# Forgetting attention in a two-layer decoder step: scores of two more heads ahead of a head's transposes, and the samples' bias in steps

## The chip, the cores and the metric

The kernel runs on one core of one Trainium2 chip. The time is device microseconds of one execution. TensorE (PE) multiplies matrices into PSUM, VectorE (DVE) and ScalarE (ACT) read PSUM and work element by element, GpSimd (POOL) works in SBUF, and SyncE (SP) holds most of the DMA queue.

## The reference

One inference step of a two-layer trunk for a prompt of 512 tokens and a group of 8 samples with 4 tokens each (544 columns in all), width 1024, float32. Layer 0 is Mamba-2 heads beside sliding-window attention; layer 1, which the change touches, is forgetting attention. Each layer ends with cross-attention into 256 memory tokens and a SwiGLU FFN. Cut to what matters here:

```python
q, k, v, logf = odd_split(hp @ w_in_odd[li], fox_fb[li])      # 16 query heads, 4 key/value heads, width 64
cum = jnp.cumsum(logf, axis=1)
bias = cq[..., :, None] - c[..., None, :]                     # logit[t,s] += cum[t] - cum[s], causal mask
p = jax.nn.softmax(s * d ** -0.5 + bias, axis=-1)             # per block of 128 queries
o = jnp.einsum('...kgqs,...skd->...qkgd', p, v)
...
kp = cache_fox_k[li, page_table]                              # samples: 8 pages of 128 keys each, gathered
lp = cache_fox_logf[li, page_table]
cum = jnp.cumsum(jnp.concatenate([lp, logf], axis=1), axis=1)
```

## The kernel before, in words

Activations lie transposed, 128 rows of the width on the partitions. A product in float32 is made of three fp32r matmuls: weights and activations are split into a high and a low part (`acc3`), and a weight piece that a DMA has put into `room` is split by ScalarE (L161, high part) and VectorE (L162, low part) into `split_t`. `linear_steps` is a generator: one step is one output piece of 128 rows for one half of the columns (256 or 288), 24 matmuls.

In `odd` the keys, values and gates are projected, then `fox_keys` stacks high and low parts of the keys with the cumulated gates (kh, kl). `fox_bias` makes the samples' bias from the cache: it gathers the log gates of 64 pages by an indirect DMA (lg), transposes them on TensorE (16 transposes) to LTS by ScalarE copies (L1169), sums them by matmuls against ones and against a strict triangle (L), adds the later pages' totals (`late`, seven small VectorE additions), and splits the result into S. Before, all of that is written ahead of the query projection of heads 0 to 7 (`linear(wq, range(4), ...)`).

`fox_prompt(q, K2, V, m, c)` then handles one block of 128 queries (c) for 8 heads (m): a head's scores are two matmuls into a PSUM bank ("sc", two banks; from the 33rd head on also one of the three "tr" banks), VectorE adds the mask, writes the result to one of four buffers in `prt` and takes the minimum (L1135), ScalarE takes the exponential and the sum (L1136), VectorE the reciprocal (L1137), GpSimd the scaling (L1138). TensorE transposes the probabilities (tag "tp", two banks), VectorE or ScalarE copy them to PT (L1144), and after eight heads TensorE multiplies them with V. There are 64 such heads, with 128 to 512 keys.

Between the heads stand steps of three other generators, by the table `FOX_PLAN`: "q" the other half of the query projection, "s" the samples' attention in four groups of two samples (`fox_sample`, whose pages of keys and values SP loads by an address from the page table, 16 DMAs of 128 KB each), and "m" the memory's keys and values for cross-attention. After them comes the output projection (wd_o).

The order that is written is a priority. A scheduler that plays the program through puts every engine's instructions in the order that stands in the program, so an engine's order differs from the written one.

Of the kernel before, what the change touches and what calls it, by code (L numbers as in the profile page):

```python
# [9 lines left out]
F32 = mybir.dt.float32  # L10
F32R = mybir.dt.float32r
# [8 lines left out]
P = 128  # L20
D = 1024
KD = 8
# [13 lines left out]
FGROUPS = ((0, 4), (4, 4), (8, 4), (12, 4), (16, 6))  # L36
NEG = -1e30

FOX_PLAN = {}
for _a, _heads in (("q", range(4, 33, 4)), ("s", [33,34,36,38,40,41,43,45,47,49,51,53,55,57,59,61]), ("m", range(34, 64, 4))):  # L40
    for _h in _heads:
# [64 lines left out]
class Net:  # L106
# [880 lines left out]
    def odd(self, st, nxt, fill):  # L987
        nc, tc, I, O = self.nc, self.tc, self.I, self.O
        with ExitStack() as es:
# [23 lines left out]
            klast = self.last  # L1013
# [28 lines left out]
            wq = self.pieces(I["wd_q"], KD)  # L1042
            with tc.tile_pool(name="fox", bufs=1) as fx:
                self.pvs = []
                self.qst, self.prt = fx.tile([P, 4352], F32R, name="qst"), fx.tile([P, 4736], F32, name="prt")
                self.fsel = self.qst[:, 4096:4352]
                self.qs_at = self.pr_at = 0
                K2 = self.fox_keys(kT, ncum)
                S, sel = self.fox_bias(fx, klast)
                self.linear(wq, range(4), KD, xh, xl, qe)  # L1050
                self.take(q)
                self.banks = ['sc']
                gens = {"q": self.linear_steps(wq, range(4, 8), KD, xh, xl, qe),
                        "s": self.fox_sample(q, kTs, Qb, ncs, V, lf, fx, S, sel), "m": fill()}
                next(gens["s"])
                heads = 0
                for m in range(2):
                    for c in range(4):
                        for _ in self.fox_prompt(q, K2, V, m, c):
                            heads += 1  # L1060
                            self.banks = ['sc'] if heads < 33 else ['sc', 'sc', 'tr']
                            for a in FOX_PLAN.get(heads, ""):
                                next(gens[a], None)
                for a in "qsm":
                    for _ in gens[a]:
                        pass
                self.hold = self.whold = self.pvs[5]
                oh, ol = Big(self, "oh1", F32R), Big(self, "ol1", F32R)
                for c in range(2):
                    o, N = CH[c]  # L1070
                    for j in range(8):
                        last = self.split(oh, ol, q[j][:, o:o + N], j, o, N)
                self.x_load(self.xd, last)
                self.cross_keys(1, last)
                st2 = nxt()
                self.linear(self.pieces(I["wo_d"], KD), range(8), KD, oh, ol, self.x_evac(st2), tail=2, lead=3)
                self.hold = self.whold = None
        return st2

    def fox_keys(self, kT, ncum):  # L1080
# [14 lines left out]
        for j in range(2):  # L1095
            Q = self.qst[:, 2048 + 1024 * j:3072 + 1024 * j].rearrange("p (r i t) -> p r i t", r=2, i=4)
            for r in range(2):
                b = 64 - 64 * r
                d = nc.vector.tensor_copy(Q[b:b + 64, r], self.cst[0:64, C_OH:C_OH + 4].unsqueeze(2).to_broadcast([64, 4, 128]))
                self.after(d, self.last)  # L1100
        mask = self.prt[:, 4224:4736]
        self.zero(mask[:, 0:384])
        self.after(nc.gpsimd.tensor_copy(mask[:, 384:512], self.cst[:, C_SWA + 128:C_SWA + 256]), self.last)
        return kh, kl
# [11 lines left out]
            nc.vector.tensor_tensor(Q[0][b, r], src, Q[0][a, r].bitcast(F32), ALU.subtract)  # L1116
        return Q

    def fox_prompt(self, q, K2, V, m, c):
        nc = self.nc  # L1120
        W = 128 * (c + 1)
        tok = slice(128 * c, 128 * c + 128)
        Q = self.fox_queries(q, m, tok)
        PT = [self.H("PT")[:, 0:2048].rearrange("p (k r i t) -> p k r i t", k=2, r=2, i=4) for _ in range(c // 2 + 1)]
        mask = self.prt[:, 4736 - W:4736]
        for r in range(2):
            for i in range(4):
                sc = self.bank([P, 512])
                for z in range(2):
                    self.mm(sc[:, 0:W], Q[z][:, r, i], K2[z][:, m, r, 0:W], z == 0, z == 1)  # L1130
                nm, den, rec = self.ty(1), self.ty(1), self.ty(1)
                self.pr_at = (self.pr_at + 512) % 2048
                pr = self.prt[:, self.pr_at:self.pr_at + 512]

                nc.vector.tensor_tensor_reduce(pr[:, 0:W], sc[:, 0:W], mask, -1.0, 1e30, ALU.add, ALU.min, nm)  # L1135
                nc.scalar.activation(pr[:, 0:W], pr[:, 0:W], AF.Exp, bias=nm, scale=-1.0, accum_out=den)  # L1136
                nc.vector.reciprocal(rec, den)  # L1137
                nc.gpsimd.tensor_scalar(pr[:, 0:W], pr[:, 0:W], rec, 1.0, ALU.mult, ALU.mult)  # L1138
                tp = self.psum("tp", [P, 4, 128])
                for kb in range(c + 1):  # L1140
                    self.tr(tp[:, kb], pr[:, 128 * kb:128 * kb + 128])
                for u in range(c // 2 + 1):
                    e = min(2, c + 1 - 2 * u)
                    (nc.scalar.copy if i % 2 else nc.vector.tensor_copy)(PT[u][:, 0:e, r, i], tp[:, 2 * u:2 * u + e])  # L1144
                yield
        pv = self.psum("pv", [P, 4, 128])
        for kb in range(c + 1):
            for r in range(2):
                g = 2 * m + r
                self.mm(pv[64 * r:64 * r + 64], V[:, kb, 64 * g:64 * g + 64], PT[kb // 2][:, kb % 2, r], kb == 0, kb == c)  # L1150
        self.pvs.append(nc.vector.tensor_copy(q.half(m)[:, :, tok], pv))  # L1151

    def fox_bias(self, fx, last):

# [3 lines left out]
        lg = self.H("lg")[0:64, 0:2048]  # L1158
        nc.gpsimd.indirect_dma_start(out=lg, out_offset=None, in_=I["fox_logf"],
                                     in_offset=bass.IndirectOffsetOnAxis(ap=pg.bitcast(U32), axis=0))  # L1160
        ll = self.H("LTS")
        LT, suf = ll[:, 0:1024], ll[:, 1024:2048]
        L4 = LT.rearrange("p (g b h) -> p h b g", g=8, b=8)
        for u in range(2):
            tp = self.psum("tp", [P, 8, 64])
            for h in range(8):
                hh = 8 * u + h
                self.tr(tp[:, h], lg[:, 128 * hh:128 * hh + 128], 64)
            nc.scalar.copy(L4[:, 8 * u:8 * u + 8], tp.rearrange("p h (b g) -> p h b g", g=8))  # L1169

        pt = self.psum("tp", [P, 8])
        for g in range(8):
            self.mm(pt[:, g:g + 1], LT[:, 128 * g:128 * g + 128], self.ones[:, 0:1], True, True)
        tot, late = (fx.tile([P, 8], F32, name=n) for n in ("tot", "late"))
        nc.vector.tensor_copy(tot, pt)
        self.after(nc.vector.memset(late, 0.0), last)
# [2 lines left out]
        for u in range(2):  # L1179
# [3 lines left out]
                self.mm(tp[:, g], LT[:, 128 * x:128 * x + 128], self.L, True, True)  # L1183
            sv = suf[:, 512 * u:512 * u + 512].rearrange("p (g k) -> p g k", g=4)
            nc.vector.tensor_tensor(sv, tp, late[:, 4 * u:4 * u + 4].unsqueeze(2).to_broadcast([P, 4, 128]), ALU.add)
        S = self.H("S", F32R)[:, 0:2048].rearrange("p (s k) -> p s k", s=2)
        for r in range(2):
            a, b = slice(64 * r, 64 * r + 64), slice(64 - 64 * r, 128 - 64 * r)
# [2 lines left out]
        sel = self.fsel.rearrange("p (a t) -> p a t", t=4)  # L1191
        i2 = self.ident[:, 0:64].unsqueeze(2).to_broadcast([P, 64, 4]), self.ident[:, 64:128].unsqueeze(2).to_broadcast([P, 64, 4])
        self.after(nc.vector.tensor_tensor(sel, i2[0], i2[1], ALU.add), last)
        return S, sel.rearrange("p a t -> p (a t)")

    def fox_sample(self, q, kTs, Qb, ncs, V, lf, fx, S, sel):

# [25 lines left out]
        for G in range(4):  # L1223
# [9 lines left out]
            for b2 in range(2):  # L1233
# [3 lines left out]
                    self.mm(sn[a:a + 32], lq, kTs[:, m], True, False)  # L1237
                a = 64 * b2
                self.mm(sn[a:a + 64], ncs.rearrange("p h t -> p (h t)"), self.ident[0:32, 0:32], False, True)
            wk = self.prt[:, 2048:4224]  # L1240
            pr = wk[:, 0:1056]
            gate = nc.vector.tensor_tensor(pr[:, 1024:1056], sn, c[:, C_MN + 32 * G:C_MN + 32 * G + 32], ALU.add)
            if G < 3:
# [576 lines left out]
```

## Time and profile before

| | us |
|---|---|
| median of 3 runs (lowest to highest) | 1713.23 (1710.82 to 1717.07) |
| the profiled execution, its own time | 1713.53 |
| its span, first to last instruction | 1711.7 |
| TensorE busy, matmuls | 1652.0 (97%) |
| TensorE weight loads | 1522.6 (89%) |
| VectorE busy | 1184.8 (69%) |
| ScalarE busy | 779.2 (46%) |
| GpSimd busy | 332.1 (19%) |
| mean granted clock of TensorE | 0.984 of full speed |

Matmuls overlap, and their ends are modelled, so that TensorE's share does not say that it runs at its peak. The sums of durations below are made against the profiled execution, 1713.53 us.

### The profile page before, as it was taken

The numbers are of one execution on the slowest core, as the hardware profiler recorded it, in microseconds if no ns is written. First come the engines' busy times: TensorE is split into PE (matmuls) and PEld (weight loads), VectorE is DVE, ScalarE is ACT, GpSimd is POOL, SyncE is SP. The second block draws the span as 40 slices with busy tenths as digits, with TensorE's granted clock in tenths as the row PEclk, the third lists the DMA queues.
The fourth block names the chain that finished last, engine by engine and source line by source line (L and its number), as shares of the span: only waits on it lengthen the run. The fifth ranks groups of instructions, "written<-read, shape, count | busy, mean of one in ns | idle before, by whom it ended". The sixth has DMA issues, their size and how long they took to land. (4 is left out here: it accounts for less than half of the span.)

```text
span 1711.7 us, 32340 instructions
## 1 busy us (share of the span) xinstructions
PE 1652.0 (97%) x12720; PEld 1522.6 (89%) x12720; DVE 1184.8 (69%) x2296; ACT 779.2 (46%) x1603; POOL 332.1 (19%) x510
## 2 busy tenths in 40 slices
PE   6999999998999999999999999988999999999998
PEld 6988899886997999999999996655998999999997
DVE  6666678876866887667676567545577877777754
ACT  4345445344545544444445245535445354444444
POOL 5022312666412300000002103111223100000002
PEclk9999999999999999999999989989999999999998
DMA  5111424136533233233213424445542232233212
GB/s 184 54 55 46 143 83 132 49 111 241 183 106 121 77 114 102 83 103 107 86 69 133 138 77 125 144 136 165 197 172 69 81 112 99 87 106 105 74 64 88
DMA packets 71221, 189.27 MB, mean 111 GB/s; under 512 B 7612, under 2 KB 34012, under 8 KB 63452
## 3 DMA queue, kind: packets, MB, share of 16 engines
q1 hardware_dynamic: 69388, 184.84, 32.6%
q8 instruction: 100, 1.64, 0.4%
q10 hardware_dynamic: 1600, 1.83, 0.4%
q0 software_dynamic: 80, 0.52, 0.1%
q14 instruction: 53, 0.43, 0.1%
HBM read 172.22 MB, written 14.95 MB: 109 GB/s over the span
## 5 line engine op out<-in xcount | busy, mean ns | idle before, releaser
L137 PE MATMUL ps<-xh,split_t 128*128 128x288 f32 (+1 forms) x2304 | 464.5, 294 | 14.8 <-ACT split_t L161 12.0
L137 PEld LDWEIGHTS ps<-xh,split_t 128*128 128x128 f32 x2304 | 370.9, 190 | 22.2 <-ACT split_t L161 12.9
L1539 PE MATMUL ps<-xf,split_t 128*128 128x272 f32 x2592 | 348.9, 289 | 3.1 <-DVE split_t L1520 2.1
L137 PE MATMUL ps<-xl,split_t 128*128 128x256 f32 (+1 forms) x1152 | 338.6, 295 | 1.3 <-DVE xl L251 1.0
L1539 PEld LDWEIGHTS ps<-xf,split_t 128*128 128x128 f32 x2592 | 335.0, 188 | 4.4 <-DVE split_t L1520 3.0
L260 POOL TENSOR_TENSOR room<-room,sq 128x256 f32<-128x256 f32 (+1 forms) x96 | 85.9, 899 | 777.3 <-ACT sq L259 775.6
L137 PEld LDWEIGHTS ps<-xl,split_t 128*128 128x128 f32 x1152 | 218.6, 190 | 6.1 <-issue 3.5
L137 PE MATMUL ps<-hh,fs 128*128 128x256 f32 (+1 forms) x1024 | 206.3, 288 | 0.0
L161 ACT CAST split_t<-room 128x1024 fp32r<-128x1024 f32 (+1 forms) x128 | 130.1, 1019 | 153.0 <-PE ps L137 107.9
L162 DVE TENSOR_TENSOR split_t<-room,split_t 128x1024 fp32r<-128x1024 f32 (+1 forms) x128 | 156.1, 1222 | 31.0 <-ACT split_t L161 29.5
L137 PEld LDWEIGHTS ps<-hh,fs 128*128 128x128 f32 x1024 | 164.9, 188 | 0.4 <-ACT fs L1583 0.4
L1520 DVE TENSOR_TENSOR split_t<-fr,split_t 128x1024 fp32r<-128x1024 f32 x108 | 131.7, 1220 | 34.2 <-ACT split_t L1519 34.2
L1519 ACT CAST split_t<-fr 128x1024 fp32r<-128x1024 f32 x108 | 113.4, 1052 | 86.7 <-PE ps L1539 52.2
L137 PE MATMUL ps<-hl,fs 128*128 128x256 f32 (+1 forms) x512 | 147.3, 288 | 0.0
L137 PE MATMUL ps<-oh,split_t 128*128 128x288 f32 (+1 forms) x512 | 103.6, 294 | 2.6 <-DVE ty L1135 1.4
L137 PEld LDWEIGHTS ps<-hl,fs 128*128 128x128 f32 x512 | 96.4, 188 | 0.0
L137 PEld LDWEIGHTS ps<-oh,split_t 128*128 128x128 f32 x512 | 81.6, 188 | 9.4 <-issue 5.4
L137 PE MATMUL ps<-ol,split_t 128*128 128x288 f32 (+1 forms) x256 | 76.5, 299 | 0.6 <-DVE ol L248 0.5
L1583 ACT CAST fs<-room 128x512 fp32r<-128x512 f32 x64 | 39.4, 618 | 82.5 <-PE ps L137 67.3
L137 PE MATMUL ps<-hh,split_t 128*128 128x256 f32 (+1 forms) x384 | 73.4, 288 | 0.0
L251 DVE SCALAR_TENSOR_TENSOR xl<-x,room,xh 128x256 fp32r<-128x256 f32 (+1 forms) x96 | 69.1, 749 | 5.9 <-ACT xh L250 5.9
L1596 DVE TENSOR_TENSOR x<-x,ps 128x256 f32<-128x256 f32 (+1 forms) x128 | 54.5, 433 | 26.6 <-PE ps L137 26.3
(423 smaller groups left out, 3109.7 us busy)
## 6 DMA issues: line engine op xcount, KB each, us to landing
fr<-wfi SPq DMA_DIRECT2D x36, 1024.0 KB
room<-wfo SPq DMA_DIRECT2D x64, 256.0 KB
room<-wo_e SPq DMA_DIRECT2D x16, 512.0 KB
xk<-mem_k SPq DMA_DIRECT2D x8, 1024.0 KB
xv<-mem_v SPq DMA_DIRECT2D x8, 1024.0 KB
room<-wfi SPq DMA_DIRECT2D x16, 512.0 KB
fox_k<-fox_k SPq DMA_DIRECT2D x64, 128.0 KB
fox_v<-fox_v SPq DMA_DIRECT2D x64, 128.0 KB
```

Of the source, the lines that this page charges most:

```text
L137: self.nc.tensor.matmul(out, lhsT, rhs, start=start, stop=stop)
L161: nc.scalar.copy(hi[:, 0:n], raw[:, 0:n])
L162: nc.vector.tensor_tensor(lo[:, 0:n], raw[:, 0:n], hi[:, 0:n].bitcast(F32), ALU.subtract)
L251: return nc.vector.scalar_tensor_tensor(ll, src, g, hh.bitcast(F32), ALU.mult, ALU.subtract)
L260: nc.gpsimd.tensor_tensor(acc, acc, sq[:, 0:N], ALU.add)
L1519: nc.scalar.copy(hi, t)
L1520: nc.vector.tensor_tensor(lo, t, hi.bitcast(F32), ALU.subtract)
L1539: self.nc.tensor.matmul(ps, w[a][:, k], x[:, b, k], start=start and k == 0 and i == 0, stop=k == 3 and i == 2, skip_group_check=True)
L1583: nc.scalar.copy(hi, raw)
L1596: nc.vector.tensor_tensor(x, x, ps, ALU.add)
```

## The change

It does two things. `fox_prompt` no longer issues a head's transposes, copies and product with V at once: it puts them on a list, and `fox_turn` issues those of a head when two younger heads' scores stand behind it (`FOX_AHEAD = 2`); the list goes on over the blocks. `prt` has a fifth buffer for that, and the parts behind it move by 512 columns. `fox_bias` becomes a generator with a `yield` behind the gather, behind each half of the transposes, behind the page sums and behind each half of the suffix sums; its steps are taken between the steps of the query projection of heads 0 to 7.

```diff
+FOX_AHEAD = 2
...
-                self.qst, self.prt = fx.tile([P, 4352], F32R, name="qst"), fx.tile([P, 4736], F32, name="prt")
+                self.qst, self.prt = fx.tile([P, 4352], F32R, name="qst"), fx.tile([P, 5248], F32, name="prt")
...
-                S, sel = self.fox_bias(fx, klast)
-                self.linear(wq, range(4), KD, xh, xl, qe)
+                bias = self.fox_bias(fx, klast)
+                next(bias)
+                for _ in self.linear_steps(wq, range(4), KD, xh, xl, qe):
+                    next(bias, None)
+                for _ in bias:
+                    pass
+                S, sel = self.fS, self.fsel
...
-                heads = 0
+                heads, ahead = 0, []
...
-                        for _ in self.fox_prompt(q, K2, V, m, c):
+                        for _ in self.fox_prompt(q, K2, V, m, c, ahead):
...
+                self.fox_turn(ahead, 0)
...
+        def turn(pr, r, i):
+            if not PT:
+                PT.extend(self.H("PT")[:, 0:2048].rearrange("p (k r i t) -> p k r i t", k=2, r=2, i=4) for _ in range(c // 2 + 1))
+            tp = self.psum("tp", [P, 4, 128])
+            for kb in range(c + 1):
+                self.tr(tp[:, kb], pr[:, 128 * kb:128 * kb + 128])
+            for u in range(c // 2 + 1):
+                e = min(2, c + 1 - 2 * u)
+                (nc.scalar.copy if i % 2 else nc.vector.tensor_copy)(PT[u][:, 0:e, r, i], tp[:, 2 * u:2 * u + e])
+            if (r, i) == (1, 3):
+                pv = self.psum("pv", [P, 4, 128])
...
-                self.pr_at = (self.pr_at + 512) % 2048
+                self.pr_at = (self.pr_at + 512) % 2560
...
-                tp = self.psum("tp", [P, 4, 128])
-                for kb in range(c + 1):
-                    self.tr(tp[:, kb], pr[:, 128 * kb:128 * kb + 128])
-                for u in range(c // 2 + 1):
-                    e = min(2, c + 1 - 2 * u)
-                    (nc.scalar.copy if i % 2 else nc.vector.tensor_copy)(PT[u][:, 0:e, r, i], tp[:, 2 * u:2 * u + e])
+                ahead.append((turn, pr, r, i))
+                self.fox_turn(ahead, FOX_AHEAD)
                 yield
...
+    def fox_turn(self, ahead, left):
+        while len(ahead) > left:
+            f, *a = ahead.pop(0)
+            f(*a)
...
+        yield
         ll = self.H("LTS")
...
             nc.scalar.copy(L4[:, 8 * u:8 * u + 8], tp.rearrange("p h (b g) -> p h b g", g=8))
+            yield
...
             self.mm(pt[:, g:g + 1], LT[:, 128 * g:128 * g + 128], self.ones[:, 0:1], True, True)
+        yield
...
             nc.vector.tensor_tensor(sv, tp, late[:, 4 * u:4 * u + 4].unsqueeze(2).to_broadcast([P, 4, 128]), ALU.add)
+            yield
...
-        return S, sel.rearrange("p a t -> p (a t)")
+        self.fS = S
```

What the scheduler makes of it on the engines, in the instructions' own order (a number after ps is the PSUM tile's; L137 and L140 before are L138 and L141 in the change):

**The bias.** TensorE before; ps_10996 is the second query piece, ps_11025 the third:

```order
L137 MATMUL ps_10996<-xh_10309,split_t 128x288
L140 MATMUL ps_10853<-room,lg_10850 128x64 x8
L140 MATMUL ps_10863<-room,lg_10850 128x64 x8
L137 MATMUL ps_10873<-room,LTS_10852 128x1 x8
L137 MATMUL ps_10893<-room,LTS_10852 128x128 x4
L137 MATMUL ps_10899<-room,LTS_10852 128x128 x4
L137 MATMUL ps_11025<-xh_10099,split_t 128x256
```

TensorE in the change, where the transposes stand in the third query piece (ps_11013):

```order
L138 MATMUL ps_11013<-xl_10100,split_t 128x256
L138 MATMUL ps_11013<-xh_10099,split_t 128x256
L141 MATMUL ps_10883<-room,lg_10850 128x64 x8
L141 MATMUL ps_10919<-room,lg_10850 128x64 x8
L138 MATMUL ps_11013<-xh_10099,split_t 128x256
```

and where the matmuls on LTS stand, in that piece's second half of the columns (ps_11045); the last four come later:

```order
L138 MATMUL ps_11045<-xh_10309,split_t 128x288 x2
L138 MATMUL ps_10958<-room,LTS_10882 128x1 x8
L138 MATMUL ps_11004<-room,LTS_10882 128x128 x4
L138 MATMUL ps_11045<-xl_10310,split_t 128x288
L138 MATMUL ps_11045<-xh_10309,split_t 128x288 x2
```

The block of bias work is now in three places of the projection. VectorE at the same place, before (the first split_t is the third query piece's low part):

```order
L1093 CAST kl_10827<-cumr_10818 32x512
L1089 TENSOR_TENSOR kl_10827<-kT_10526,kh_10826 64x2x512
L162 TENSOR_TENSOR split_t<-room,split_t 128x1024 x2
L1175 COPY tot<-ps_10873 128x8
L1178 TENSOR_TENSOR late<-late,tot 128x1 x7
L1185 TENSOR_TENSOR LTS_10852<-ps_10893,late 128x512
L1185 TENSOR_TENSOR LTS_10852<-ps_10899,late 128x512
L455 SCALAR_TENSOR_TENSOR q_1093_10939<-ps_10914,room 128x256
```

and in the change:

```order
L1100 CAST kl_10827<-cumr_10818 32x512
L456 SCALAR_TENSOR_TENSOR q_1086_10880<-ps_10855,room 128x256
L456 SCALAR_TENSOR_TENSOR q_1086_10880<-ps_10893,room 128x288
L456 SCALAR_TENSOR_TENSOR q_1086_10880<-ps_10932,room 128x256
L1096 TENSOR_TENSOR kl_10827<-kT_10526,kh_10826 64x2x512
L163 TENSOR_TENSOR split_t<-room,split_t 128x1024
L456 SCALAR_TENSOR_TENSOR q_1086_10880<-ps_10967,room 128x288
L163 TENSOR_TENSOR split_t<-room,split_t 128x1024
```

Three evacuations of q have moved ahead of the third piece's low part.

**The late heads.** TensorE before, at the 54th to the 58th head (scores are kh and kl against qst, transposes are prt against room, S against qst is the bias of the last group of samples):

```order
L137 MATMUL ps_13400<-kh_10826,qst 128x384
L137 MATMUL ps_13400<-kl_10827,qst 128x384
L137 MATMUL ps_13674<-kh_10826,qst 128x512
L137 MATMUL ps_13674<-kl_10827,qst 128x512
L137 MATMUL ps_13431<-kh_10826,qst 128x384
L137 MATMUL ps_13431<-kl_10827,qst 128x384
L140 MATMUL ps_13249<-room,prt 128x128 x3
L137 MATMUL ps_13447<-S_10905,qst 128x512
L140 MATMUL ps_13283<-room,prt 128x128 x3
```

and in the change:

```order
L138 MATMUL ps_13546<-kh_10826,qst 128x512
L138 MATMUL ps_13546<-kl_10827,qst 128x512
L141 MATMUL ps_13271<-room,prt 128x128 x3
L141 MATMUL ps_13278<-room,prt 128x128 x4
L138 MATMUL ps_13293<-kh_10826,qst 128x384
L138 MATMUL ps_13293<-kl_10827,qst 128x384
L138 MATMUL ps_13388<-kh_10826,qst 128x384
L138 MATMUL ps_13388<-kl_10827,qst 128x384
L141 MATMUL ps_13284<-room,prt 128x128 x4
```

Before, two more heads' scores stand directly ahead of the first row shown. In the change transposes stand between. SP's queue in the change, between the third group's values and the last group's keys:

```order
L1237 DMA fox_v_12923<-fox_v 128x256
L1233 ISA x2
L1232 DMA tab_13009<-pages 1x16
L158 DMA room<-wo_d 128x1024 x2
L1233 TENSOR_LOAD tab_13009
L1233 ISA x2
```

Before, those two DMAs of wo_d's weights stand behind the last group's keys.

**The end of the stage.** TensorE before, from the last head's transposes (oh, ol: the output projection's operands):

```order
L140 MATMUL ps_13733<-room,prt 128x128 x4
L137 MATMUL ps_13902<-ol_1542_13754,split_t 128x288
L137 MATMUL ps_13902<-oh_1541_13753,split_t 128x288 x2
L137 MATMUL ps_13902<-ol_1542_13754,split_t 128x288
L137 MATMUL ps_13902<-oh_1541_13753,split_t 128x288 x2
L137 MATMUL ps_13740<-PT_13497,odd 64x512 x3
```

and in the change:

```order
L138 MATMUL ps_13902<-oh_1541_13753,split_t 128x288
L141 MATMUL ps_13726<-room,prt 128x128 x4
L141 MATMUL ps_13733<-room,prt 128x128 x4
L138 MATMUL ps_13740<-PT_13556,odd 64x512 x3
L138 MATMUL ps_13740<-PT_13557,odd 64x512 x4
```

The projection's matmuls behind the last transposes have moved ahead of the last two heads' transposes.

## Rows read from the trace of the kernel before

**Rows 1.** The page, busy time of TensorE: us (share of the span) xinstructions.

```profile
PE 1652.0 (97%) x12720; PEld 1522.6 (89%) x12720; DVE 1184.8 (69%) x2296; ACT 779.2 (46%) x1603; POOL 332.1 (19%) x510
```

**Rows 2.** Stretches of 20 us: length, busy us (xinstructions) per engine, granted clock, DMA.

```profile
980.00:1000.00 20.00, 16.51 (x103) 14.66 (x102) 8.85 (x18) 11.07 (x13) 0.01 (x1) 0.83 0.33 95
1000.00:1020.00 20.00, 20.00 (x151) 20.00 (x151) 14.37 (x28) 7.53 (x12) 0.38 (x1) 0.92 0.13 33
...
1040.00:1060.00 20.00, 18.05 (x106) 12.80 (x104) 16.29 (x53) 11.69 (x32) 8.23 (x15) 1.00 0.45 132
1060.00:1080.00 20.00, 17.37 (x94) 8.62 (x92) 14.87 (x50) 12.28 (x36) 7.49 (x12) 1.00 0.24 78
...
1120.00:1140.00 20.00, 18.55 (x89) 10.72 (x91) 10.35 (x32) 7.30 (x19) 2.89 (x6) 0.85 0.50 153
1140.00:1160.00 20.00, 17.08 (x195) 11.39 (x194) 10.19 (x45) 10.84 (x32) 4.60 (x8) 0.91 0.39 124
```

**Rows 3.** Timeline, TensorE, 989 to 1002: start us, us, engine, line, what [idle before].

```profile
989.47 1.22 PE L140 MATMUL ps<-room,lg 64*128 64x64 f32 x16
994.17 7.19 PE L137 MATMUL ps<-room,LTS 128*128 128x1 f32 x32 [3.49 <-ACT LTS L1169]
1001.02 0.56 PE L137 MATMUL ps<-xh,split_t 128*128 128x256 f32 x1
```

**Rows 4.** Stretches within the same 22 us, columns as in rows 2.

```profile
994.20:1001.00 6.80, 6.80 (x32) 6.80 (x33) 1.98 (x9) 0.00 (x0) 0.00 (x0) 0.50 0.26 78
1001.00:1003.30 2.30, 2.30 (x13) 2.30 (x13) 1.90 (x5) 1.05 (x1) 0.00 (x0) 0.51 0.03 7
1003.30:1016.00 12.70, 12.70 (x104) 12.70 (x103) 8.76 (x14) 5.63 (x7) 0.00 (x0) 1.00 0.13 41
```

**Rows 5.** Timelines of ScalarE and VectorE around the third query piece.

```profile
987.64 1.05 ACT L161 CAST split_t<-room 128x1024 fp32r<-128x1024 f32 x1
...
986.77 0.42 DVE L1093 CAST kl<-cumr 32x512 fp32r<-32x512 f32 x1
987.23 1.22 DVE L1089 TENSOR_TENSOR kl<-kT,kh 64x1024 fp32r<-64x1024 f32 x1
988.72 1.23 DVE L162 TENSOR_TENSOR split_t<-room,split_t 128x1024 fp32r<-128x1024 f32 x1 [0.27 <-ACT split_t L161]
...
1002.01 1.47 DVE L455 SCALAR_TENSOR_TENSOR q<-ps,room 128x256 f32<-128x256 f32 x4
```

**Rows 6.** TensorE's waits, 980 to 1220: us in total, times, longest us.

```profile
PE ps L137 <- DVE ty L1135: 8.3, 12, 1.4
...
PE ps L137 <- DMA fox_k<-fox_k: 1.2, 2, 0.9
```

**Rows 7.** Timeline, TensorE, second half of the heads: its longer waits.

```profile
1122.19 0.80 PE L137 MATMUL ps<-S,qst 128*128 128x512 f32 x1 [0.76 <-DVE ty L1135]
...
1151.29 0.44 PE L137 MATMUL ps<-kh,qst 128*128 128x384 f32 x1 [1.20 <-DVE ty L1135]
...
1162.84 1.05 PE L137 MATMUL ps<-fox_k,odd 128*32 128x512 f32 x4 [0.91 <-DMA fox_k<-fox_k]
...
1180.41 0.50 PE L137 MATMUL ps<-kh,qst 128*128 128x512 f32 x1 [1.08 <-DVE ty L1135]
...
1184.25 0.39 PE L137 MATMUL ps<-oh,split_t 128*128 128x256 f32 x1 [1.37 <-DVE ty L1135]
...
1202.99 0.40 PE L137 MATMUL ps<-oh,split_t 128*128 128x288 f32 x1 [1.25 <-ACT oh L245]
```

**Rows 8.** Timeline, SP's queue: last group of samples, table and keys.

```profile
1144.01 0.32 SPq L1208 DMA_DIRECT2D tab<-pages  x1
...
1155.19 9.25 SPq L1213 DMA_DIRECT2D fox_k<-fox_k  x16
```

**Rows 9.** SP's queue, waits 1010 to 1215, columns as in rows 6.

```profile
SPq L157 <- DVE split_t L162: 22.3, 4, 16.6
```

**Rows 10.** Timeline, ScalarE: the last head's copies.

```profile
1196.68 0.65 ACT L1144 COPY PT<-ps 128x256 f32<-128x256 f32 x2 [0.75 <-PE ps L140]
```

More of the change, by code (lines that the diff above doesn't have):

```diff
@@ L1100, in fox_keys @@
                 self.after(d, self.last)
-        mask = self.prt[:, 4224:4736]
+        mask = self.prt[:, 4736:5248]
         self.zero(mask[:, 0:384])
@@ L1117, in fox_queries, with fox_prompt @@
         return Q
-    def fox_prompt(self, q, K2, V, m, c):
+    def fox_prompt(self, q, K2, V, m, c, ahead):
         nc = self.nc
@@ L1123, in fox_prompt @@
         Q = self.fox_queries(q, m, tok)
-        PT = [self.H("PT")[:, 0:2048].rearrange("p (k r i t) -> p k r i t", k=2, r=2, i=4) for _ in range(c // 2 + 1)]
-        mask = self.prt[:, 4736 - W:4736]
+        PT = []
+        mask = self.prt[:, 5248 - W:5248]
+        def turn(pr, r, i):
[9 more added lines that the diff above has]
+                pv = self.psum("pv", [P, 4, 128])
+                for kb in range(c + 1):
+                    for r in range(2):
+                        g = 2 * m + r
+                        self.mm(pv[64 * r:64 * r + 64], V[:, kb, 64 * g:64 * g + 64], PT[kb // 2][:, kb % 2, r], kb == 0, kb == c)
+                self.pvs.append(nc.vector.tensor_copy(q.half(m)[:, :, tok], pv))
         for r in range(2):
@@ L1138, in fox_prompt @@
                 nc.gpsimd.tensor_scalar(pr[:, 0:W], pr[:, 0:W], rec, 1.0, ALU.mult, ALU.mult)
-                tp = self.psum("tp", [P, 4, 128])
-                for kb in range(c + 1):
-                    self.tr(tp[:, kb], pr[:, 128 * kb:128 * kb + 128])
-                for u in range(c // 2 + 1):
-                    e = min(2, c + 1 - 2 * u)
-                    (nc.scalar.copy if i % 2 else nc.vector.tensor_copy)(PT[u][:, 0:e, r, i], tp[:, 2 * u:2 * u + e])
-                yield
[L1146 to L1151, printed above, removed]
+                ahead.append((turn, pr, r, i))
+                self.fox_turn(ahead, FOX_AHEAD)
+                yield
+    def fox_turn(self, ahead, left):
+        while len(ahead) > left:
+            f, *a = ahead.pop(0)
+            f(*a)
     def fox_bias(self, fx, last):
@@ L1239, in fox_sample @@
                 self.mm(sn[a:a + 64], ncs.rearrange("p h t -> p (h t)"), self.ident[0:32, 0:32], False, True)
-            wk = self.prt[:, 2048:4224]
+            wk = self.prt[:, 2560:4736]
             pr = wk[:, 0:1056]
```

## The prediction

> **What bounds the kernel now.** I read the page first. TensorE is busy for 1652.0 of 1711.7 us [rows 1], so a change of this size can only give back what TensorE idles, or runs at the low clock, in the stage that it touches: layer 1's forgetting attention, from about 980 to 1205 us. The table by stretches of 20 us [rows 2] shows there what is to be had. From 980 to 1000 TensorE is busy for 16.51 of 20 us and the granted clock is 0.83; from 1000 to 1020 it is 0.92. From 1040 to 1080 it idles 1.95 and 2.63 us at full clock, and from 1120 to 1160 it idles 1.45 and 2.92 us at a clock of 0.85 and 0.91.
>
> Then the timeline of TensorE around the samples' bias [rows 3]. The sixteen transposes of the gathered log gates start at 989.47; the first matmul on LTS starts at 994.17, after 3.49 us in which TensorE waited for ScalarE's copy of them; the projection of the queries goes on at 1001.02. All matmuls on LTS run at a granted clock of 0.50, which is the 1.2 GHz level, and so does the projection until about 1003.3; from there on it is 2.4 GHz [rows 4]. TensorE had idled 3.49 us just before the clock fell.
>
> Last the waits. Over the stage TensorE waited 8.3 us in 12 places for the reduction on VectorE (L1135) that reads a score bank, and 1.2 us in two places for pages of keys [rows 6]. The longest of the former stand in the second half of the heads: 0.76, 1.20, 1.08 and 1.37 us [rows 7].
>
> **The bias in steps.** Before, the bias takes TensorE from 989.47 to 1001.02, 11.55 us [rows 3]. In the new order the same sixteen transposes stand inside the third piece of the projection, and the matmuls on LTS come some 22 projection matmuls later, so that the projection covers ScalarE's copy. What must stay is the transposes' 1.22 us and the LTS matmuls at full clock, 7.19 / 2 = 3.60 us [rows 3, 4]: 4.82 us. That gives 6.73 us, and with the clock kept up the projection from 1001.0 to 1003.3 wins half of its 2.3 us [rows 4], 1.15 us: 7.9 us in all.
>
> The bias also covered something. The third query piece, which now starts at 989.25, needs its low part from VectorE (L162). Before, that ran from 988.72 to 989.95, while TensorE was on the bias [rows 5]. In the new order VectorE has three evacuations of q in front of it, of the kind that took 1.47 us for four [rows 5], 0.37 us each, or 1.1 us. The evacuations start when the last small copy of kl ends, 987.19; then come the 1.22 us of L1089 and the 1.23 us of L162 [rows 5]: 987.19 + 1.1 + 1.22 + 1.23 = 990.7, against a need at some 989.4 after two matmuls on the high part (which ScalarE has done by 988.7, [rows 5]). I take 1.5 us of a new wait with the semaphores. It leaves 6.4 us. The bounds: 7.9 us without that wait, and 3.4 us if the copy's wait comes back for 3 us besides it. The split of the fourth piece has over 5 us of projection in front of its use, and the first scores, which need VectorE's work on the queries and now have S's two subtractions in front of it, still have about 2 us of slack by the same counting: both at nothing, and about 1 us of TensorE each if that cover is too short.
>
> **The heads.** The diff puts the scores of two heads between a head's scores and its transposes, but in the old order the scores of the fifth head already stand ahead of the first head's transposes, and from the 18th to the 32nd head both orders alternate score and transpose with four heads between. So I book nothing for the first half. There a score waits for its bank's reader on VectorE, which is busy for 16.29 and 14.87 of 20 us [rows 2], and no traced order changes that. In the second half the old order has bursts: five scores in a row, then the transposes; the new one has two or three scores, then transposes. A third score in a row finds neither of the two banks read. Four such waits make 4.41 us [rows 7]. I take 3.0 us of it, since shorter bursts remain; the bounds are 0 and 4.41, and 4.41 lost if the new order sets as many of its own. The fifth buffer of prt and the shifted offsets cost no instruction.
>
> **The end of the stage.** Before, six projection matmuls stand between the last head's transposes and the matmuls with V that need their copies; the new order has nothing between. The copies take 0.65 us [rows 10]. I book 0.7 us lost; bounds 0 and 1.25, the wait that the output projection has there now [rows 7].
>
> **Sum.** -6.4 - 3.0 + 0.7 = -8.7 us. Against the profiled execution's own 1713.53 us that is 1704.8; that execution lies 0.3 us above the median of the runs, so the forecast is 1704.5 us. Half a per cent, about what a measurement of this kernel can tell from no change, is 8.6 us: the forecast stands just at that line.
>
> **Rivals.**
> 1. *The low clock of the second half goes too.* With shorter waits the clock may not fall between 1100 and 1160. At 0.85 and 0.91, 30% and 18% of 20 us are at the lower level, and half of that is lost: 3.0 + 1.8 = 4.8 us [rows 2]. For it: the episodes begin where waits crowd. Against: the sample's small matmuls and its pages are still there. It gives 1697 to 1702, about 1700. The Trainium skill speaks for more here: its Perfetto Trace Analysis, in "Identifying the Most-Contended Engine", calls matmul busy time a poor measure because matmuls are pipelined, and wants the weight loads' share. By that rule 1040 to 1060 would have 20 - 12.80 = 7.20 us of room instead of 1.95, and the heads alone could give over 10 us. The heads' matmuls are up to 512 columns wide on one weight load, so a low share is their shape and I take the rule at no more than this rival's chance.
> 2. *Pages set the pace.* SP's queue is one stream: for the last group of samples it issues the page table at 1144.01, its first page of keys only at 1155.19, and sixteen take 9.25 us [rows 8]; TensorE waited for that group 0.91 us [rows 7]. If TensorE comes earlier by 6 us the same loads become its wait, at the third and fourth group, and the gain of the heads goes into them with some of the bias's: 1707 to 1712.
> 3. *The heads part does nothing*, because the scheduler had the lead already: 1713.2 - 6.4 + 0.7 = 1707.5, and up to 1710.5 with the bias at its lower bound.
> 4. *Slower: weights in front of pages.* In SP's new order two pieces of wd_o's weights (room<-wo_d) stand between the last page table and the last group's keys; before, they stood behind the keys. Such an issue waits until the split (L162) has freed its slot, and one of those waits in this stage was 16.6 us long [rows 9]. If the slot is late, every page behind it is late, TensorE stands at the group's scores and then runs at 1.2 GHz as it did after the bias: 16.6 + about 5 us (10 us at half speed, as in rows 4) - 8.7 = 13 us slower, 1718 to 1727. It decides from a wait of some 12 us on; SP reaches that place only after the third group's values, when the pieces before should long be split, so it is unlikely.
>
> **How the numbers follow.** Forecast 0.49 (1701 to 1708, of which 0.29 below the line and 0.20 above), first rival 0.17, second 0.18, third 0.09, fourth 0.07. Faster by over 0.5% is 0.29 + 0.17 = 0.46, within 0.5% is 0.20 + 0.18 + 0.09 = 0.47, slower 0.07. The range reaches from the first rival's low end, 1697, to the second's high end, 1712; it leaves out the fourth and the ends of the unknown costs.
>
> **What would show it.** Right: after, the clock stays at 1.00 from 980 to 1020, the wait for ScalarE's copy of LTS is gone, one wait of 1 to 2 us for L162 stands before the third query piece, and waits for L1135 sum to about 5 us. Wrong: the waits move to fox_k or to L162 with several us each, the granted clock falls at another place after them, or the first scores start less than 5 us earlier against the projection's progress.

## The result and the profile after

The changed kernel takes 1695.6 us (median of 4 runs, 1692.2 to 1699.4) against 1713.5 us: a ratio of 0.9895, interval 0.9862 to 0.9928, or 17.9 us less. That is more than half a per cent, about twice the forecast's 8.7 us, and just below the forecast's range. Run again beside its variants it took 1695.7 us, ratio 0.9888 (0.9870 to 0.9907). The profiled execution has a span of 1696.9 us (own time 1698.67), 14.8 us less than before.

The stretches of 20 us of the changed kernel, to be read against [rows 2]; columns as there:

```profile
980.00:1000.00 20.00, 20.00 (x159) 18.71 (x158) 11.77 (x25) 12.26 (x14) 0.09 (x1) 1.00 0.31 82
1000.00:1020.00 20.00, 20.00 (x164) 20.00 (x163) 16.55 (x42) 10.86 (x23) 2.47 (x6) 1.00 0.41 132
1100.00:1120.00 20.00, 19.49 (x142) 13.25 (x142) 10.27 (x38) 9.07 (x26) 3.38 (x7) 0.91 0.52 149
1120.00:1140.00 20.00, 19.16 (x140) 10.57 (x143) 9.18 (x29) 8.08 (x23) 1.77 (x3) 1.00 0.68 208
1140.00:1160.00 20.00, 18.59 (x124) 9.14 (x115) 12.71 (x43) 9.56 (x29) 3.64 (x6) 1.00 0.52 151
1160.00:1180.00 20.00, 16.79 (x159) 13.76 (x160) 10.02 (x36) 11.12 (x30) 4.87 (x7) 0.91 0.45 131
```

At the bias TensorE is busy all of the time and at 1.00. In the second half of the heads it is busier, and the low clock of 0.85 and 0.91 between 1120 and 1160 is gone; 0.91 is left in two stretches (from 1100 to 1120 the kernel before had 0.90).

TensorE's timeline at the bias, against [rows 3]: transposes, matmuls on LTS in two pieces, the first scores, nothing waiting:

```profile
989.69 1.22 PE L141 MATMUL ps<-room,lg 64*128 64x64 f32 x16
...
994.85 2.84 PE L138 MATMUL ps<-room,LTS 128*128 128x1 f32 x24
...
999.19 1.05 PE L138 MATMUL ps<-room,LTS 128*128 128x128 f32 x8
...
1008.89 0.22 PE L138 MATMUL ps<-kh,qst 128*128 128x128 f32 x1
```

TensorE's waits from 980 to 1205, against [rows 6]:

```profile
PE ps L138 <- DVE ty L1160: 4.8, 10, 0.7
PE ps L141 <- ACT sO L1296: 3.1, 1, 3.1
PE ps L138 <- ACT oh L246: 1.2, 1, 1.2
PE ps L141 <- POOL prt L1163: 0.9, 2, 0.6
```

The wait for LTS and the four waits for L1135 in [rows 7] are gone; the longest wait for a score's reduction (L1160 here) is 0.7 us, and behind the 33rd head these waits sum to 0.7 us, where they summed to 5.6. A new one stands in second place, 3.1 us for ScalarE's copy of the samples' output (L1296).

**Where the 14.8 us lie.** To compare kernels I measure along the work, from the first matmul on cumw (979.25 before, 978.41 after) to the first score's reduction on VectorE, to the 33rd head's, and to the second half of the output projection, the row with 1.25 us in [rows 7], which every kernel here has. In us; "idle" is TensorE's waiting and "low" the time at the lower clock level, both from the 33rd reduction to the end, and some low time falls on waits:

| kernel | to 1st | 1st to 33rd | 33rd to end | idle | low |
|---|---|---|---|---|---|
| before | 39.1 | 57.7 | 126.9 | 12.5 | 13.7 |
| e_bias | 33.6 | 57.9 | 133.0 | 15.3 | 20.5 |
| e_fill | 35.0 | 57.6 | 127.6 | 12.8 | 13.7 |
| e_ahead1 | 33.6 | 56.8 | 131.4 | 14.2 | 23.9 |
| e_first | 33.6 | 56.8 | 130.1 | 13.4 | 17.1 |
| e_heads | 38.1 | 57.1 | 118.2 | 8.8 | 3.4 |
| the change | 33.6 | 56.8 | 119.4 | 8.6 | 6.8 |
| again | 33.6 | 56.8 | 119.2 | 8.3 | 6.8 |
| e_ahead3 | 33.6 | 55.6 | 117.8 | 11.8 | 3.4 |
| e_second | 33.6 | 56.8 | 114.1 | 5.5 | 0 |
| q_pool | 33.5 | 56.8 | 114.0 | 6.9 | 0 |

(q_again agrees with q_pool, q_pool3 with e_ahead3, to 0.1 us in each stretch.) From before to the change: 5.5 us up to the first score, 0.9 in the first half, 7.5 in the second, and 0.8 from ahead of the stage. In the second half 3.9 us of the gain are idle time. For the clock, only low time in which TensorE works counts, since the rest is in the idle time already. In the kernel before that is 8.75 and 3.22 us of the two low stretches there:

```profile
1115.91:1126.15 10.24, 8.75 (x29) 4.06 (x28) 5.30 (x23) 5.40 (x17) 1.93 (x4) 0.50 0.32 98
1153.46:1156.87 3.41, 3.22 (x13) 2.08 (x12) 2.08 (x9) 1.99 (x6) 1.18 (x2) 0.50 0.11 38
```

In the change TensorE works through all of its 6.8 us. At half speed half of such time is lost: 6.0 us before, 3.4 after, so 2.6 us of the gain are the clock's. About 1 us of the 7.5 is left to neither.

### The profile page after: what moved, and what is told of

It reads as the page before. It is cut to its first block, busy times and chain, and to the rows that moved or that the text cites. A ratio compares the mean times of both kernels' runs of the same rounds, so it can differ in the third digit from the quotient of the medians.

```text
span 1696.9 us, 32362 instructions
## 1 busy us (share of the span) xinstructions
PE 1645.9 (97%) x12720; PEld 1518.7 (89%) x12720; DVE 1184.0 (70%) x2296; ACT 778.3 (46%) x1603; POOL 328.3 (19%) x510
## 4 chain that ended last, share of the span: by engine, by line
PE 91%; DVE 3%; POOL 2%; ACT 1%; issue 1%; DMA 1%; SPq 0%; DVEq 0%; POOLq 0%; ACTq 0%
PE ps L138 66%; PE ps L1563 22%; PE ps L141 3%; POOL room L425 1%; DMA room<-wo_d 0%; POOL sq L421 0%; DVE split_t L1544 0%; ACT prt L1161 0%; DVE prt L1160 0%; DVE xs L879 0%; ACT split_t L162 0%; DMA mem<-mem 0%; DVE meml L252 0%; DVE x L1730 0%; DMA x<-x 0%
## 5 line engine op out<-in xcount | busy, mean ns | idle before, releaser
L138 PE MATMUL ps<-xh,split_t 128*128 128x288 f32 (+1 forms) x2304 | 463.8, 294 | 13.8 <-ACT split_t L162 11.8
L138 PEld LDWEIGHTS ps<-xh,split_t 128*128 128x128 f32 x2304 | 371.1, 190 | 19.8 <-ACT split_t L162 12.8
L138 PE MATMUL ps<-xl,split_t 128*128 128x256 f32 (+1 forms) x1152 | 339.1, 295 | 1.2 <-DVE xl L252 1.0
L138 PEld LDWEIGHTS ps<-xl,split_t 128*128 128x128 f32 x1152 | 218.9, 190 | 6.9 <-issue 4.3
L138 PE MATMUL ps<-hh,fs 128*128 128x256 f32 (+1 forms) x1024 | 206.3, 288 | 0.0
L162 ACT CAST split_t<-room 128x1024 fp32r<-128x1024 f32 (+1 forms) x128 | 130.3, 1019 | 156.5 <-PE ps L138 112.3
L138 PEld LDWEIGHTS ps<-hh,fs 128*128 128x128 f32 x1024 | 164.9, 188 | 0.4 <-ACT fs L1607 0.4
L138 PE MATMUL ps<-hl,fs 128*128 128x256 f32 (+1 forms) x512 | 147.3, 288 | 0.0
L138 PE MATMUL ps<-oh,split_t 128*128 128x288 f32 (+1 forms) x512 | 105.7, 298 | 1.3 <-ACT oh L246 1.2
L138 PEld LDWEIGHTS ps<-hl,fs 128*128 128x128 f32 x512 | 96.4, 188 | 0.0
L138 PEld LDWEIGHTS ps<-oh,split_t 128*128 128x128 f32 x512 | 83.2, 192 | 8.3 <-issue 5.0
L138 PE MATMUL ps<-ol,split_t 128*128 128x288 f32 (+1 forms) x256 | 77.1, 301 | 0.3 <-DVE ol L249 0.2
L138 PE MATMUL ps<-hh,split_t 128*128 128x256 f32 (+1 forms) x384 | 73.4, 288 | 0.0
```

The source lines that it names most:

```text
L138: self.nc.tensor.matmul(out, lhsT, rhs, start=start, stop=stop)
L162: nc.scalar.copy(hi[:, 0:n], raw[:, 0:n])
```

## The experiments

**The two parts, each alone.** e_bias takes from the change's diff only the generator `fox_bias` and its loop; e_heads keeps the rest and drains the bias first:

```diff
-                bias = self.fox_bias(fx, klast)
-                next(bias)
-                for _ in self.linear_steps(wq, range(4), KD, xh, xl, qe):
-                    next(bias, None)
-                for _ in bias:
+                for _ in self.fox_bias(fx, klast):
                     pass
+                self.linear(wq, range(4), KD, xh, xl, qe)
```

> The kernel before with the bias in steps alone: its loop and its generator as in the change, the heads, the four score buffers and the order of scores and transposes as before. By the prediction's sum this is -6.4 us (-7.9 without the new wait for the third query piece, which the trace of the change does not show): 1705.5 to 1707, first scores some 6 to 7 us earlier than before. By the theory that the heads' gain (the trace of the change: some 7.5 us in the second half) comes from the shorter bursts, the rest of the stage keeps its waits for VectorE of 0.8 to 1.4 us after five scores in a row and its low clock between 1100 and 1160, and the time is 1705 to 1707. By the rival that the second half gains because the whole stage comes 7 us earlier against the pages and the weights, the second half gains here as well: 1696 to 1700.

> The change with its bias drained whole ahead of the queries' projection, as before, and with its order of the heads. By the prediction's sum: -3.0 + 0.7 = -2.3 us, 1711. By the theory that shorter bursts take both the waits and the low clock of the second half: -7 to -8 us, 1705 to 1707, with the low clock and the 3.5 us wait at the bias still there and no wait over 0.8 us for the reduction in the second half. By the rival that only the two parts together give the second half's gain: 1710 to 1713.

Measured: e_bias 1709.4 us, ratio 0.9981 (0.9970 to 0.9991); e_heads 1699.8 us, 0.9925 (0.9907 to 0.9943); before beside them 1713.7. So the heads alone give 13.9 us where I had 2.3 us, beyond what even the theory of the bursts (several heads' scores in a row) expected, and the bias gives 4.3 us alone and 4.1 us on top of the heads (1699.8 to 1695.7). The parts add up, within intervals of some 3 us to either side. In e_heads's profile 10.4 us of the gain lie in this stage and 5.1 us ahead of it, where the order of the engines' instructions is that of the kernel before, so that those 5.1 us are not the change's. The bias does bring the first score 5.5 us forward, but in e_bias's profile the second half, still with its bursts, is 6.1 us longer than before. Its two stretches with a low clock:

```profile
1100.00:1120.00 20.00, 16.75 (x60) 10.95 (x60) 7.82 (x30) 6.74 (x20) 2.40 (x5) 0.66 0.50 157
...
1160.00:1180.00 20.00, 14.84 (x80) 10.25 (x79) 13.93 (x40) 12.45 (x32) 2.90 (x5) 0.83 0.64 207
```

**How deep the lookahead.** One head, and three with a sixth buffer:

```diff
-FOX_AHEAD = 2
+FOX_AHEAD = 1
```

> The change with scores of one more head, not two, between a head's scores and its transposes (five buffers kept). Its traced order still has bursts of five and six scores in the second half, as before. By the theory of the bursts the second half gains nothing: 1705 to 1708, as with the bias in steps alone. By the rival that any lead of the scores over the transposes, or the fifth buffer, or the place of the matmuls with V gives the gain: 1696 to 1700.

> The change with scores of three more heads between a head's scores and its transposes, and a sixth buffer for them. The bursts stay short in the second half (two or three scores). By the theory of the bursts it is as the change: 1694 to 1698. By the rival that the depth itself gives the gain (more time for the softmax between scores and transposes) it is a few us faster than the change, 1690 to 1694; by the prediction's fear of work at the end of the stage with nothing behind it, three heads to turn there cost up to 1 us more: 1697 to 1699.

Measured: e_ahead1 1706.7 us, 0.9963 (0.9950 to 0.9976); e_ahead3 1693.0 us, 0.9881 (0.9867 to 0.9895). One head of lookahead leaves the scheduler's bursts of five and six scores, and the second half stays long, though the fifth buffer and the new place of the matmuls with V are there. Such a burst in e_ahead1's trace, with no transposes between; each row has a matmul on kl behind it, and the granted clock is 0.50 from 1080.1 to 1090.4:

```profile
1076.80 0.31 PE L138 MATMUL ps<-kh,qst 128*128 128x128 f32 x1
...
1079.08 0.33 PE L138 MATMUL ps<-kh,qst 128*128 128x128 f32 x1 [1.87 <-ACT prt L1276]
...
1080.00 0.22 PE L138 MATMUL ps<-kh,qst 128*128 128x128 f32 x1
...
1080.18 0.42 PE L138 MATMUL ps<-kh,qst 128*128 128x128 f32 x1
...
1080.93 0.54 PE L138 MATMUL ps<-kh,qst 128*128 128x256 f32 x1
...
1083.82 0.47 PE L138 MATMUL ps<-kh,qst 128*128 128x128 f32 x1 [2.15 <-DVE ty L1160]
```

Three heads are not told apart from two by the runs, though 1693.0 lies where the rival of depth had it; in the profile the first half is 1.2 us shorter (55.6), in q_pool3's too.

**Which half.** The lookahead in one half of the heads only (e_second; e_first has the two values exchanged):

```diff
-                self.fox_turn(ahead, FOX_AHEAD)
+                self.fox_turn(ahead, FOX_AHEAD if m else 0)
```

> The change with its lookahead of two heads in the second half of the heads alone (33 to 64); in the first half each head is turned at once. By the traces so far the first half (first to 33rd reduction: 57.7 us before, 56.8 in the change, 57.9 with the bias in steps alone) is worth 1 us at most and the second half (126.9 us before, 119.4 in the change) carries the rest: 1695 to 1698. Rival, that the lookahead must be there from the first head to keep VectorE fed: 1700 or more.

> The mirror of it: two heads of lookahead in heads 1 to 32 alone, none from head 33 on, so that the traced order of the second half has its bursts of five and six scores again. Theory that those bursts cost the time: 1706 to 1710, like the bias in steps alone (1709.4), with two or three low-clock stretches and some 12 us or more of idle TensorE between the 33rd head and the end. Rival, that the first half carries the gain: 1696 to 1699.

Measured: e_second 1692.9 us, 0.9891 (0.9873 to 0.9908); e_first 1707.1 us, 0.9971 (0.9960 to 0.9982). The first half takes 56.8 us in both. With lookahead in the second half there is no low clock in it at all (114.1 us); without, it is back at 130.1 us. That e_second is 5.3 us shorter there than the change, with the same lookahead, I had not expected: its weights go out in another order, it has no wait for sO (on which more below), and its longest wait inside the second half is 1.8 us for fox_v. Between all these kernels the order of the loads turns together with that of the heads, and no run holds it fixed. In the kernel before only 1.2 of the 12.5 us idle are put down to loads, so the larger part should be the bursts'; how much they are worth alone is not shown. The same stretch, e_first's, then e_second's:

```profile
1100.00:1120.00 20.00, 15.81 (x75) 8.97 (x65) 6.74 (x28) 5.34 (x18) 1.52 (x4) 0.70 0.56 172
```

```profile
1100.00:1120.00 20.00, 19.87 (x146) 12.75 (x146) 9.72 (x36) 8.98 (x26) 3.36 (x7) 1.00 0.50 157
```

**Is it the idle time that lets the clock fall?** The kernel before, its bias where it was, with matmuls in the wait for LTS that nothing reads (`last_t` is the last transpose, `kfill` the high part of the keys):

```diff
-                self.tr(tp[:, h], lg[:, 128 * hh:128 * hh + 128], 64)
+                last_t = nc.tensor.transpose(tp[:, h], lg[:, 128 * hh:128 * hh + 128], self.ident[0:64, 0:64])
...
+        jk = self.psum("pv", [P, 512])
+        for _ in range(15):
+            self.after(nc.tensor.matmul(jk, self.kfill[:, 0, 0, 0:128], self.kfill[:, 0, 0, 0:512], start=True, stop=True), last_t)
         pt = self.psum("tp", [P, 8])
...
```

> The kernel before, with fifteen matmuls of 512 columns on the prompt's keys, whose results nothing reads, behind the sixteen transposes of the gathered log gates (some 3.2 us at full clock, inside the 3.49 us in which TensorE waits for ScalarE's copy). They take the idle time away without taking anything off the path. Theory that the idle time is what lets the clock fall: the matmuls on LTS and the projection behind them run at 1.00, the first scores come some 5 us earlier (half of the 10.2 us at the lower level), and the time is 1707 to 1709. Rival, that the small transposes and matmuls of the bias themselves lower the clock: it falls all the same, 1713 to 1715. The scheduler turns some scores and transposes of the second half by this edit; if that decides, the time moves with the waits there.

Measured: 1708.4 us, 0.9967 (0.9954 to 0.9980). TensorE's timeline, and the clock over the matmuls on LTS:

```profile
986.77 1.22 PE L1169 MATMUL ps<-room,lg 64*128 64x64 f32 x16
987.92 3.72 PE L1174 MATMUL ps<-kh 128*128 128x512 f32 x15
991.61 3.84 PE L137 MATMUL ps<-room,LTS 128*128 128x1 f32 x32
```

```profile
991.60:995.40 3.80, 3.80 (x34) 3.79 (x34) 1.29 (x8) 0.00 (x0) 0.00 (x0) 1.00 0.49 142
```

The matmuls on LTS take 3.84 us where they took 7.19 [rows 3, 4], with the same work and no work saved: the idle time was the cause here, not the bias's small matmuls. Filling the wait with work that is thrown away gained 4.9 us, as much as moving the bias (4.3 us) within the intervals.

**The new wait.** In the change, the third weight piece of the output projection stands in SyncE's queue behind the last group's 32 pages. SyncE's queue, then ScalarE, then TensorE:

```profile
1129.56 0.83 SPq L158 DMA_DIRECT2D room<-wo_d  x2
1133.00 16.13 SPq L1237 DMA_DIRECT2D fox_k<-fox_k  x16
1149.38 11.80 SPq L1237 DMA_DIRECT2D fox_v<-fox_v  x16
1161.29 0.85 SPq L158 DMA_DIRECT2D room<-wo_d  x2
```

```profile
1167.35 1.04 ACT L162 CAST split_t<-room 128x1024 fp32r<-128x1024 f32 x1 [3.05 <-DMA room<-wo_d]
...
1169.53 0.38 ACT L1296 ACTIVATE sO<-ps,ty 128x128 f32<-128x128 f32 x1
```

```profile
1169.96 0.33 PE L141 MATMUL ps<-room,sO 128*128 128x128 f32 x1 [3.12 <-ACT sO L1296]
```

TensorE's wait is put down to L1296, but that copy only stood behind ScalarE's split of weights that had not landed. q_pool issues the third piece from GpSimd's queue (q_pool3: the first three, with three heads of lookahead):

```diff
-        d = nc.sync.dma_start(raw[:, 0:n], src)
+        d = (dma or nc.sync).dma_start(raw[:, 0:n], src)
...
-                self.linear(self.pieces(I["wo_d"], KD), range(8), KD, oh, ol, self.x_evac(st2), tail=2, lead=3)
+                self.linear(lambda n: self.wpiece(I["wo_d"][n], KD, 128, nc.gpsimd if n in (2,) else None), range(8), KD, oh, ol, self.x_evac(st2), tail=2, lead=3)
```

> The changed kernel unchanged, beside its variants on one chip. From the runs so far (median 1695.6, the lookahead alone 1699.8, three heads of lookahead 1693.0) it should lie at 1694 to 1698; the theory that the bias in steps is worth some 4 us, with the lookahead as without it (1713.7 to 1709.4 without), says 1695 to 1696; by the prediction's 6.4 to 7.9 us it would lie at 1692 to 1693.

> The changed kernel with the third piece of the output projection's weights (wo_d) issued from GpSimd's queue instead of SyncE's, where 32 pages of the last group stand ahead of it (SyncE issues it at 1161.29, ScalarE then waits 3.05 us for it to land, and TensorE 3.12 us for ScalarE's copy of the samples' output behind that). Theory that this queue makes the wait: it goes, and the low clock of 3.4 us right behind it with it: 3.1 + 1.7 = 4.8 us, 1690 to 1692. Rival, that another piece or page is then late instead, or that GpSimd, which scales the probabilities, waits for the weights' slot: 1695 to 1698 or more.

> Three heads of lookahead with a sixth buffer, and the first three pieces of wo_d issued from GpSimd's queue. Theory of the queue: ScalarE's 3.1 us wait for the weights goes (it stands there with three heads of lookahead as well), 1689 to 1691. Rival, that its cost there was small (TensorE then waited 1.1 us on it) or that GpSimd stands on the slot: 1692 to 1696.

> The kernel with the third piece of wo_d on GpSimd's queue once more (1691.8 in its first session, the change 1695.7 in the same), to see whether its lead over the change holds: 1690 to 1694 if the removed waits (ScalarE's 3.05 us and the low clock behind it) are the cause, 1694 to 1697 if the first session was luck with the clock.

Measured: q_pool 1691.8 us, 0.9875 (0.9855 to 0.9896), and 1692.7 us, 0.9880 (0.9862 to 0.9898) when run again. The piece now leaves at 1135.11; along the work (this stage begins 3.8 us sooner in q_pool's profile) that is 22 us earlier than in the change, and ScalarE waits 1.00 us for it:

```profile
1135.11 0.62 POOL L158 DMA_DIRECT2D room<-wo_d  x1 [1.55 <-DVE ty L1162]
```

```profile
1139.17 1.05 ACT L162 CAST split_t<-room 128x1024 fp32r<-128x1024 f32 x1 [1.00 <-DMA room<-wo_d]
```

The wait for sO is gone, the low clock behind it (from 1171.7 in the change) with it, and the second half is over 5 us shorter than the change's, in both of its profiles. Not all of that is the moved piece's: the change's other low time, 3.4 us from 1100.0 on, lies some 40 us ahead of the place where the two kernels' matmuls part, and is missing in q_pool as well (see the last section). By the medians q_pool lies 3 to 4 us ahead of the change; the intervals of the ratios overlap, so the runs alone don't tell the two apart. The Trainium skill (DMA: Bandwidth & Descriptors, "Issuing engines are not separate DMA queues") says that transfers from several issuing engines share the same DMA engines, and that issuing from another saves only the time to issue. Here that time, with what stands ahead in the queue, was 22 us.

q_pool3 took 1693.0 us, 0.9885 (0.9865 to 0.9904): no better than e_ahead3. There the weights' loads go out among the last group's keys, and TensorE waits for those instead:

```profile
1134.37 1.05 PE L138 MATMUL ps<-fox_k,odd 128*32 128x512 f32 x4 [3.14 <-DMA fox_k<-fox_k]
```

## Why the prediction was wrong, step by step

**The late heads, -3.0 us: the step that failed.** It booked four waits and nothing for the clock that falls behind such waits; that was priced at 4.8 us, but set aside as a rival with a chance of 0.17. The second half gained 7.5 us in the profile (8.7 in e_heads'), 3.9 by idle and 2.6 by the clock. The waits were too small as well: those for a score's reduction fell by 4.9 us, not 3.0, and other waits shrank too; 3.1 us of that went into the new wait for sO, which no term had. Of the four rows added up to 4.41 us, two stand ahead of a prompt's score, one ahead of the samples' bias and one ahead of the output projection. The direction was right: where the bursts stay the second half stays long (e_ahead1, e_first), where they are short it is short (e_second). The argument against the rival, that the sample's small matmuls and pages would keep the clock low, fell: e_second and q_pool have both and no low clock in the second half. Of 17.8 us in the runs the clock has at most 10.4: a span times the missing share of its clock is 24.0 us before (median of 15 runs) and 13.6 us in the change (of 5, beside them), low time on which TensorE waits included. In the two profiles, waits left out, the stage has 21.1 us of work at the lower level before (9.1 at the bias [rows 4], 12.0 in the second half) and 6.8 after: half of the difference is 7.1 of 14.8 us.

**The bias, -6.4 us.** The first scores come 36.57 us after cumw before and 30.48 after: 6.09 us, with 14 projection matmuls (1.55 us by their columns at 2.4 GHz) more ahead of them, so 7.6 us, close to the 7.9 us of the working. Before, the two rows are

```profile
979.25 3.60 PE L137 MATMUL ps<-cumw 128*128 128x512 f32 x8
...
1015.82 0.23 PE L137 MATMUL ps<-kh,qst 128*128 128x128 f32 x1
```

Two things went otherwise:

- The 1.5 us for a new wait were booked on a misread row. The split at 988.72 in [rows 5] is that of the fourth query piece; the third's had run at 976.67, and the list of VectorE's order ahead of the prediction takes the fourth's for the third's in the same way. In the change they stand at

```profile
975.83 1.21 DVE L163 TENSOR_TENSOR split_t<-room,split_t 128x1024 fp32r<-128x1024 f32 x1
988.79 1.23 DVE L163 TENSOR_TENSOR split_t<-room,split_t 128x1024 fp32r<-128x1024 f32 x1
```

  and TensorE starts the third piece without a wait:

```profile
988.65 0.28 PE L138 MATMUL ps<-xl,split_t 128*128 128x256 f32 x1
```

- Work that TensorE does earlier was counted as time won at the end. The first half of the heads doesn't run at TensorE's pace: with the bias in steps alone it takes 57.9 us against 57.7, and TensorE idles 5.7 us in it against 4.1, so that the 14 matmuls done earlier buy nothing there. With that the bias is worth 4.3 us in the runs, alone, and 4.1 us with the lookahead. That the change stands 6.4 us ahead by the 33rd head, the very sum forecast for the bias, is partly luck, since 0.9 us of it are not the bias's.

**The first half, nothing:** nearly right, 0.9 us. Dropping the lookahead there (e_second) leaves it at 56.8 us, so the 0.9 us are not the lookahead's; what e_second has there and e_bias lacks is the fifth buffer and the later claim of PT, and which of them it is stays open.

**The end of the stage, +0.7 us:** the matmuls with V wait 0.46 us for their copies at 1183.25; right in kind and small.

**The rivals.** The first, the low clock going too, came nearest; its 1700 us were still too high. The weights' rule beside it gave a good number for the heads alone (over 10 us; e_heads gave 13.9 in the runs and 10.4 in this stage by its profile), but not by the room it saw: from 1040 to 1060 the weight loads are busy for only 8.04 of 20 us in the change, and that half of the heads won 0.9 us. The second, pages, did not come with this change (no wait for fox_k is left in it), but does in e_ahead3 (1.6 us at the longest) and q_pool3. The third fell. The fourth had the right loads, weights and pages in one queue, and the wrong order: the two pieces of wo_d ahead of the keys went out in 0.83 us, and it was the piece behind the pages that cost 3.1 us.

**The signs.** The clock of 1.00 from 980 to 1020, the end of the wait for LTS and about 5 us of waits for the reduction (4.8) came as said; the wait for L162 ahead of the third query piece did not, and a new wait of 3.1 us with a fall of the clock behind it, a sign of being wrong, did.

**What stays open.** Why the second half with bursts is longer still when the bias is out of the way (130.1 to 133.0 us in three profiles against 126.9 and 127.6 with the bias in a block): the low time is longer there, but idle time in sum does not set it, as e_ahead3 shows (11.8 us idle, 3.4 low). e_bias's profile shows a stage no shorter than before's (what it gains lies ahead of the stage, where nothing was changed), while its runs are 4.3 us faster; with one profile each that is not settled.

## What to carry to other kernels

Price a wait of TensorE also with the half-speed time that may follow it, as a bound of the range and not at nothing, and look at the rows by stretches for where that was: in the second half here it was worth 2.6 us beside 3.9 us of waits. A lookahead that the scheduler already finds by itself is worth nothing; look at the order it really sets, and add the lead only where it lets scores pile up against their banks. When a wait is put down to a copy, see what that copy's engine did before: it may stand behind weights in another queue.

## What was not expected of the hardware

The clock fell behind a single short wait, and behind the same wait it did not fall. In the change TensorE was busy for 0.29 us of the stretch from 1099 to 1100, with one wait of 0.71 us, and no other in the 10 us before; from 1100.0 to 1103.4 it ran at the 1.2 GHz level:

```profile
1099.00:1100.00 1.00, 0.29 (x3) 0.10 (x2) 1.00 (x2) 0.91 (x3) 0.00 (x0) 1.00 0.91 252
1100.00:1101.00 1.00, 1.00 (x5) 0.84 (x5) 0.53 (x3) 1.00 (x6) 0.00 (x0) 0.51 1.15 152
```

The second profile of the change has the same wait (0.71 us at 1097.14) and the same fall. q_pool's TensorE has the very same matmuls in the same order up to 1145 and the same wait, and there the clock stayed:

```profile
1096.09 0.38 PE L138 MATMUL ps<-kh,qst 128*128 128x256 f32 x1 [0.70 <-ACT prt L1276]
```

```profile
1096.00:1097.00 1.00, 0.78 (x5) 0.60 (x6) 0.58 (x2) 1.00 (x6) 0.00 (x0) 1.00 1.23 183
1097.00:1098.00 1.00, 1.00 (x6) 0.35 (x4) 0.82 (x4) 0.68 (x3) 0.00 (x0) 1.00 0.57 115
```

It stayed in q_again and e_heads too, behind 0.71 and 0.70 us, and in e_second behind 1.8 us for fox_v. What decides between the two no run here shows; the 1.7 us that such a fall costs (half of 3.4) belong to no kernel for certain.

Two executions of the same program agree in this stage to 0.2 us (209.7 and 209.6 for the change, 204.4 and 204.3 for q_pool), while the time ahead of the stage differs by 2.8 and 3.5 us. For these two kernels the spread of the whole time thus comes mostly from elsewhere, and a stage measured along its own work may tell kernels apart that the runs' medians don't.
